# A hybrid decoder layer on one core: the GLA values' way into token rows, and two sets of loads

## The chip, the cores and the metric

The kernel runs on one core of one Trainium2 chip. The metric is the time of one launch on the device in microseconds (us); the median of the runs is compared. One execution was also recorded by the hardware profiler, and all times inside the kernel are from that one, counted from the start of its span. The engines are named as the profile names them: PE (TensorE's matmuls), PEld (its weight loads), DVE (VectorE), ACT (ScalarE), POOL (GpSimd) and SP (SyncE, which here only issues transfers).

## What is computed

One inference step of one layer of a hybrid decoder, for a prompt group (1 x 256 tokens) and a sample group (8 sequences x 4 tokens) that share all weights. The kernel keeps both groups side by side as T = 288 columns, so each weight is read once. Cut to what matters:

```python
p_mem_k, p_mem_v = _mem_kv(mem_prompt, norm_mem, w_ck, w_cv)     # 256 memory tokens, 4 heads x 512
xn = _rmsnorm(x, norm_mix)
z, xbc, dt_raw, q, k, v, r, g_lr, gate_a, gate_b = _split(xn @ w_in, IN_SIZES)
# branch a: causal conv and SSD scan of xbc (4 groups), gated by silu(z), normed, @ w_ssd_out
# branch b: GLA, 4 heads of 256 keys and 512 values, in chunks of tokens:
att = where(mask, einsum('bihk,bjhk->bhij', qe, ke), 0)
o = einsum('bhij,bjhv->bihv', att, v) + einsum('bihk,bhkv->bihv', qe, S)
S = exp(last) * S + einsum('bjhk,bjhv->bhkv', kd, v)
#           o normed, times silu(r), @ w_gla_out
merged = sigmoid(gate_a) * branch_a + sigmoid(gate_b) * branch_b
h = x + merged @ w_mix_out
h = h + cross_attend(rmsnorm(h), memory keys, memory values) @ w_co
h = h + (silu(gt) * a) @ w_down        # a, gt: causal conv of rmsnorm(h) @ w_up, 2 x 5632 channels
```

Outputs are y of both groups and the new states, memory keys and values among them.

## The kernel before

Everything is fp32. A projection (`proj_w`) streams its weights: SP loads 512 KB at a time into the tile `raw` (a ring of 3), ACT rounds it to `whi` (`wsplit`, L103), DVE takes the rest as `wlo` (L105; both rings hold WB = 5 tiles of two k-tiles each), and PE multiplies `whi` with the high and the low half of the activations and `wlo` with the high half (L147, L148, L151; 12 matmuls of 128x288 for a tile of weights and 256 output columns). Activations stand with channels on the partitions and tokens in the columns.

The kernel goes through these stages:

1. **Memory stage** (about the first 180 us). The memory's keys and values, one head of each at a time, by `mem_proj`: weights in `raw` as before, matmuls of 128x512 at L321, L322 and L325, 6 for a k-tile. The first of the eight projections also transposes the memory's rows. Over the next four (`w_cv` 0, `w_ck` 1, `w_cv` 1, `w_ck` 2, 64 k-tiles) `weave` runs a background, one of its steps for about each k-tile: `x_norm` (37 steps) and `x_prep`. `x_norm` loads the tokens x by `x_load(n)` (L387): n = 0 the sample group, 4 transfers of 64 KB; n = 1 to 4 each 64 tokens of the prompt, 4 transfers of 128 KB. They go through SP's queue, between the weights' loads. At step 12 and at every third step from 15 to 36 `square` reads one loaded piece on ACT and turns it on DVE (L396, L398).
2. **Eight units**: four SSD groups, then four GLA heads. The background of unit n is the scan of group or head n, and its main stream is the projections of unit n + 1 and the output projection of unit n - 1; the last unit's main stream is half of gate a. `weave` mixes them by step counts (`N_MAIN`, `N_BG`). `gla_proj` of head h makes `vT` (512 values x 288 tokens, four 128-row tiles, copied out of PSUM at L978) in the first 16 steps of the unit ahead. `gla_scan` needs the prompt's values with tokens on the partitions: per 128 tokens PE transposes four 128x128 blocks (L1068), ACT copies the PSUM tile twice (`vth`, `vt`) and DVE takes `vtl`. These feed the state update (L1132) and the output (L1140).
3. **Half gate**: gate b over all 16 tiles of channels. `gate_b(t)` combines gate, branch b (`mb`) and the merged half that lies in DRAM (`mar`, four tiles a load, a ring of 2; L1334 reads it). After every fourth tile it starts a load of keys for the cross-attention. The x that the next projection adds (`hx`, two tiles a load, a ring of 3) is loaded here too.
4. `w_mix_out`, cross-attention, `w_co`, and the ConvFFN, which fills the span from about 1590 us.

The transfers of stage 3, `vT`'s new ones and the states go through POOL's queue: POOL works through its instructions in order, and a transfer that waits for its buffer holds those behind it. So does SP. The order on each engine comes from a scheduler that works on the program as recorded; `keep_in_program_order` and the background's steps bind it.

The SSD scan already has what the change brings to GLA: `load_square` reads a state in pieces of 32 rows (four transfers of 64 KB, each in runs of 32 numbers) into `sqr`, and one DVE transpose (L881), which turns every 32x32 block by itself, finishes the turn.

Of the kernel before, what the change touches and what calls it, by code (L numbers as in the profile page):

```python
# [16 lines left out]
P = 128  # L17
D = 2048
KT = D // P
SEQ = 256  # L20
# [22 lines left out]
def hybrid_step(ctx: ExitStack, tc: tile.TileContext, I: dict, O: list):  # L43
# [22 lines left out]
    def mm_tile():  # L66
        return ps.tile([P, 512], F32, tag="mm", bufs=3, name="mm")
# [204 lines left out]
    with pool("p0") as p0:  # L272
# [118 lines left out]
        def x_norm():  # L391
            ss = p0.tile([P, 9], F32, name="ss")

            def square(b):
                junk = p0.tile([P, 512], F32, name="junk")
                tc.keep_in_program_order(S.activation(junk, xrow[:, b, :], ACT.Square, accum_out=ss[:, b:b + 1]))  # L396
                tc.keep_in_program_order(
                    V.transpose(xT[:, :, 32 * b:32 * b + 32], xrow[:, b, :].rearrange("p (x j) -> p j x", j=KT)))  # L398

            for step in range(37):  # L400
                if step == 3 or step % 6 == 0 and 6 <= step <= 24:
                    x_load(step // 6)
# [175 lines left out]

    def b2r(name):
        return pa.tile([P, 512], F32R, tag="b2", bufs=10, name=name)  # L580

    def r2(name):
        return pa.tile([P, 512], F32R, tag="r2", bufs=3, name=name)
# [390 lines left out]
    def gla_proj(h, out):  # L974
        vT, sr = a4("vT"), a4("sr")
        for j2 in range(2):
            def consv(j, a, j2=j2):
                S.copy(vT[:, 2 * j2 + j, :], a)  # L978
            yield from proj(I["w_in"], O_V + 512 * h + 256 * j2, 256, X, KT, consv)
        for j2 in range(2):  # L980
            def consr(j, a, j2=j2):
                silu2(a, sr[:, j2 * 2 + j, :])
# [57 lines left out]
        out.append((eb, qe, ke, kd, kde, vT, sr))  # L1040

    def gla_scan(h, eb, qe, ke, kd, kde, vT, sr):

        sq = pa.tile([P, T], F32, tag="sq", bufs=1, name="sqa")
        sins = []
# [15 lines left out]
        ksr = rep4(kd[:, :, SEQ:T], "ksr")  # L1061
        ker = rep4(ke[:, :, SEQ:T], "ker")

        vt = []
        for i in range(2):
            a = mm_tile()
            for t in range(4):
                TR(a[:, t * P:(t + 1) * P], vT[:, t, i * P:(i + 1) * P], ident)  # L1068
            vt.append((b2r("vth"), b2r("vtl"), b2("vt")))
            split(*vt[i][0:2], a)  # L1070
            S.copy(vt[i][2], a)
            yield

        a = mm_tile()
        for i, (t0, n) in enumerate(TOK):
            for k in range(2):
# [41 lines left out]
        kt = b2r("kth"), b2r("ktl")  # L1118
        split(*kt, a)
        yield  # L1120
        elp = pa.tile([P, 2], F32, tag="elp", bufs=1, name="elp")
        V.tensor_tensor(elp, eb[:, :, 191], eb[:, :, 255], ALU.mult)
        for k in range(2):
# [198 lines left out]
    pc_cm = pool("pc")  # L1322
    pc = pc_cm.__enter__()
    mas = []
    for q in range(4):
        m = pc.tile([P, 4, T], F32, tag="mar", bufs=2, name="mar")
        G.dma_start(out=m, in_=mg_d[:, 4 * q:4 * q + 4, :])
        mas.append(m)

    def gate_b(t, a):  # L1330
        th = pc.tile([P, T], F32, tag="th", bufs=3, name="th")
# [1 line left out]
        V.scalar_tensor_tensor(th, th, 1.0, mb[:, t, :], ALU.add, ALU.mult)  # L1333
        V.tensor_tensor(th, th, mas[t // 4][:, t % 4, :], ALU.add)  # L1334
        split_from(*mx(t), th, 0.5)
        if t % 4 == 3:
            key_load(0, t // 4, th[:, 0:1])

    hx = []

    def load_x(j2):
        m = pc.tile([P, 2, T], F32, tag="hx", bufs=3, name="hx")
        G.dma_start(out=m, in_=x_d[256 * j2:256 * j2 + 256].rearrange("(t p) n -> p t n", p=P))
        hx.append(m)

    for j2 in range(3):
        load_x(j2)
    run(gate(O_GB, gate_b))
    def sq_add(acc, ht, t):

# [512 lines left out]
```

## Time and profile before

| | |
|---|---|
| median of 3 runs | 2512.9 us (2511.34 to 2514.22) |
| the profiled execution's own time | 2508.11 us |
| its span, first to last instruction | 2506.4 us |
| mean granted TensorE clock | 0.999 |
| DVE, ACT, POOL busy | 71%, 54%, 16% |
| DMA | 524 MB, mean 209 GB/s |

The profile gives busy time by engine and by group of instructions (line, engine, operation, output<-input), what ended each engine's waits, and the chain of work that ended last, followed back from the end. Ends of matmuls are modelled, so PE counts as busy over the time in which results drain; the chain is the better measure of what a matmul costs, since its pieces follow each other without overlap. An engine's name with a q is its sequencer, which issues.

### The profile page before, as it was taken

To read this page: it belongs to the slowest core of one execution; us is meant where nothing else is said; L and a number is where in the kernel's file an instruction comes from. 1 tells how busy PE (TensorE), PEld (TensorE's weight loads), DVE (VectorE), ACT (ScalarE), POOL (GpSimd) and SP (SyncE) were. 2 spreads that over 40 slices of the span, in tenths; PEclk is the share of its full clock that TensorE was granted. 3 is DMA by queue.
4 is the path that set the end of the run, shared out by engine and by line. 5 is a ranking of instruction groups with operands and counts; after the bars stand their busy time and mean duration, and the time that the engine had idled before them with its cause. 6 is when DMAs were issued, how large, how long until landed. Compare 5 with 4: busy or idle time off the path is not lost.

```text
span 2506.4 us, 50377 instructions
## 1 busy us (share of the span) xinstructions
PE 2486.2 (99%) x18858; PEld 2400.7 (96%) x18858; DVE 1768.8 (71%) x3780; ACT 1341.4 (54%) x2725; POOL 407.7 (16%) x750
## 2 busy tenths in 40 slices
PE   9999999999999999999999999999999999999998
PEld 7889999999999999999999989999999999999998
DVE  6756777797877666776666577667777677675766
ACT  6655647656464656454555544555555455454545
POOL 3002133342300000010001122402111001020012
PEclk9999999999999999999999999999999999999999
DMA  8776587867858585767678598655555555555555
GB/s 249 242 221 196 172 250 207 234 192 236 233 187 286 182 254 175 249 218 262 200 227 272 191 321 323 205 162 178 170 171 170 170 169 171 169 172 170 170 173 170
DMA packets 443189, 524.31 MB, mean 209 GB/s; under 512 B 27404, under 2 KB 390764, under 8 KB 442912
## 3 DMA queue, kind: packets, MB, share of 16 engines
q1 hardware_dynamic: 408000, 422.34, 54.8%
q0 software_dynamic: 34912, 98.74, 12.3%
q8 instruction: 148, 2.42, 0.4%
q14 instruction: 97, 0.79, 0.1%
q10 hardware_dynamic: 32, 0.01, 0.0%
HBM read 474.31 MB, written 46.66 MB: 208 GB/s over the span
## 4 chain that ended last, share of the span: by engine, by line
PE 94%; DMA 2%; DVE 2%; issue 0%; ACT 0%; SPq 0%; POOL 0%; DVEq 0%; ACTq 0%
PE acc L148 28%; PE acc L147 27%; PE acc L151 27%; PE acc L321 2%; PE acc L322 2%; PE acc L325 2%; DMA raw<-in_w_cv_dram 1%; DVE wlo L105 1%; PE mm L1168 1%; PE la L1159 1%; PE la L1492 1%; DMA raw<-in_w_co_dram 0%; PE la L1550 0%; PE mm L1132 0%; PE la L867 0%
## 5 line engine op out<-in xcount | busy, mean ns | idle before, releaser
L103 ACT CAST whi<-raw 128x512 fp32r<-128x512 f32 x1464 | 896.3, 618 | 997.5 <-PE acc L148 762.2
L105 DVE TENSOR_TENSOR wlo<-raw,whi 128x512 fp32r<-128x512 f32 x1464 | 996.7, 687 | 579.6 <-ACT whi L103 565.9
L147 PE MATMUL acc<-xn,whi 128*128 128x288 f32 (+1 forms) x1936 | 544.5, 297 | 0.5 <-DVE sz L636 0.5
L148 PE MATMUL acc<-xn,whi 128*128 128x288 f32 (+1 forms) x1936 | 541.5, 295 | 0.0
L151 PE MATMUL acc<-xn,wlo 128*128 128x288 f32 (+1 forms) x1936 | 410.1, 293 | 0.0
L148 PE MATMUL acc<-hf,whi 128*128 128x288 f32 x1408 | 393.2, 296 | 0.0
L147 PE MATMUL acc<-hf,whi 128*128 128x288 f32 x1408 | 389.1, 292 | 0.0
L147 PEld LDWEIGHTS acc<-xn,whi 128*128 128x128 f32 (+1 forms) x1936 | 364.1, 188 | 8.0 <-issue 3.9
L148 PEld LDWEIGHTS acc<-xn,whi 128*128 128x128 f32 (+1 forms) x1936 | 364.2, 188 | 4.0 <-issue 1.7
L151 PEld LDWEIGHTS acc<-xn,wlo 128*128 128x128 f32 (+1 forms) x1936 | 310.4, 188 | 1.9 <-issue 0.8
L151 PE MATMUL acc<-hf,wlo 128*128 128x288 f32 x1408 | 294.8, 290 | 0.0
L148 PEld LDWEIGHTS acc<-hf,whi 128*128 128x128 f32 x1408 | 264.9, 188 | 0.1
L147 PEld LDWEIGHTS acc<-hf,whi 128*128 128x128 f32 x1408 | 264.2, 188 | 0.1
L151 PEld LDWEIGHTS acc<-hf,wlo 128*128 128x128 f32 x1408 | 226.3, 188 | 0.0
L148 PE MATMUL acc<-pr,whi 128*128 128x288 f32 x704 | 196.6, 296 | 0.0
L147 PE MATMUL acc<-pr,whi 128*128 128x288 f32 x704 | 194.8, 293 | 0.0
L151 PE MATMUL acc<-pr,wlo 128*128 128x288 f32 x704 | 147.4, 290 | 0.0
L147 PE MATMUL acc<-un,whi 128*128 128x288 f32 x512 | 143.7, 297 | 0.0
L148 PE MATMUL acc<-un,whi 128*128 128x288 f32 x512 | 143.2, 295 | 0.0
L1664 POOL COPY fsp<-fst 128x16 f32<-128x16 f32 x88 | 36.1, 413 | 657.1 <-DVE av L1676 433.5
L148 PEld LDWEIGHTS acc<-pr,whi 128*128 128x128 f32 x704 | 132.5, 188 | 0.0
L147 PEld LDWEIGHTS acc<-pr,whi 128*128 128x128 f32 x704 | 132.1, 188 | 0.0
(523 smaller groups left out, 4295.0 us busy)
## 6 DMA issues: line engine op xcount, KB each, us to landing
raw<-in_w_in_dram SPq DMA_DIRECT2D x240, 512.0 KB
raw<-in_w_up_dram SPq DMA_DIRECT2D x176, 512.0 KB
raw<-in_w_down_dram SPq DMA_DIRECT2D x88, 512.0 KB
raw<-in_w_cv_dram SPq DMA_DIRECT2D x32, 512.0 KB
raw<-in_w_ssd_out_dram SPq DMA_DIRECT2D x32, 512.0 KB
sin<-in_state_gla_dram POOLq DMA_DIRECT2D x32, 512.0 KB, 6.1
out_dram<-sin SPq DMA_DIRECT2D x32, 512.0 KB
raw<-in_w_gla_out_dram SPq DMA_DIRECT2D x32, 512.0 KB
```

The lines of the kernel that those rows point to most:

```text
L103: S.copy(hi, raw)
L105: V.tensor_tensor(lo, raw, hi, ALU.subtract)
L147: MM(a, hi[:, k, cs], xh, start=(k0 + s0 + k == 0), stop=False)
L148: MM(a, hi[:, k, cs], xl, start=False, stop=False)
L151: MM(a, lo[:, k, cs], xh, start=False, stop=(k0 + s0 + k == nk - 1))
L321: MM(accs[m], mn_hi[:, kk, ms_], hi[:, 0, :], start=(kk == 0), stop=False)
L322: MM(accs[m], mn_lo[:, kk, ms_], hi[:, 0, :], start=False, stop=False)
L325: MM(accs[m], mn_hi[:, kk, ms_], lo[:, 0, :], start=False, stop=(kk == KT - 1))
L1159: MM(osa[NS * j:NS * j + NS, :], qdm[:, k, b, :], sins[b][:, k, :], start=False, stop=(q == 1 and k == 0))
L1168: MM(a, kb[:, k * P:(k + 1) * P], vst, start=True, stop=True)
L1492: MM(ssc[NS * c:NS * c + NS, 0:P], xq[:, j, u, :], kt[:, j], start=(j == 0), stop=(j == 15))
L1664: G.tensor_copy(sp[:, :, 0:2], st.rearrange("p (b k) -> p b k", k=2))
```

## The change

Three edits. In the memory stage `x_load(0)` to `x_load(4)` stand at steps 5, 9, 15, 21 and 27 where they stood at 3, 6, 12, 18 and 24. In each GLA head, `vT`'s prompt half is written to DRAM (512 KB, one transfer) after its projection, read back as two tiles in eight transfers of 64 KB, each of 32 partitions with runs of 32 numbers, and turned on DVE in place; PE's transposes and ACT's plain copies go, and the split stands behind the key's instead of at the scan's start. In the half gate, `mar` 0 is loaded as before, `mar` 1 after gate tile 0, and 2 and 3 after tiles 3 and 7; `hx` 0 to 2 after tiles 5, 9 and 13. Each of these loads is tied by a POOL copy of one column of the gate tile into the buffer.

```diff
             for step in range(37):
-                if step == 3 or step % 6 == 0 and 6 <= step <= 24:
-                    x_load(step // 6)
+                if step in (5, 9, 15, 21, 27):
+                    x_load((step - 3) // 6)
...
+    def dumped(x, name):
+        d = dram.tile([4 * P, SEQ], F32, name=name)
+        G.dma_start(out=d.rearrange("(t p) n -> p t n", p=P), in_=x[:, :, 0:SEQ])
+        return d
+
+    def square_load(d, name):
+        got = []
+        for i in range(2):
+            t = b2(name)
+            rows = d.rearrange("(b p) (i q j) -> i q p b j", p=32, q=4, j=32)[i]
+            for q in range(4):
+                tc.keep_in_program_order(G.dma_start(
+                    out=t[32 * q:32 * q + 32].rearrange("p (b j) -> p b j", j=32), in_=rows[q]))
+            got.append(t)
+        return got
...
+        vd = dumped(vT, f"v_d{h}")
...
-        vt = []
-        for i in range(2):
-            a = mm_tile()
-            for t in range(4):
-                TR(a[:, t * P:(t + 1) * P], vT[:, t, i * P:(i + 1) * P], ident)
-            vt.append((b2r("vth"), b2r("vtl"), b2("vt")))
-            split(*vt[i][0:2], a)
-            S.copy(vt[i][2], a)
-            yield
-
+        vs = square_load(vd, "vt")
...
         split(*kt, a)
         yield
+        vt = []
+        for i in range(2):
+            V.transpose(vs[i], vs[i])
+            vt.append((b2r("vth"), b2r("vtl"), vs[i]))
+            split(*vt[i][0:2], vs[i])
+            yield
...
+    def load_mix(q, after=None):
         m = pc.tile([P, 4, T], F32, tag="mar", bufs=2, name="mar")
+        if after is not None:
+            G.tensor_copy(m[:, 0, 0:1], after)
         G.dma_start(out=m, in_=mg_d[:, 4 * q:4 * q + 4, :])
...
         split_from(*mx(t), th, 0.5)
+        if t == 0:
+            load_mix(1, th[:, 0:1])
         if t % 4 == 3:
+            if t < 11:
+                load_mix(t // 4 + 2, th[:, 0:1])
             key_load(0, t // 4, th[:, 0:1])
...
-    for j2 in range(3):
-        load_x(j2)
+        if t in (5, 9, 13):
+            load_x(t // 4 - 1, th[:, 0:1])
```

What becomes of the order, at three places. First SP's queue in the memory stage, from the first `w_cv` projection on; `raw` are weights, `xrow` the tokens. Before:

```order
L114 DMA raw<-in_w_cv_dram 128x2x512 x3
L387 DMA xrow<-in_x_sample_dram 32x512 x4
L114 DMA raw<-in_w_cv_dram 128x2x512
L387 DMA xrow<-in_x_prompt_dram 32x2x512 x4
L114 DMA raw<-in_w_cv_dram 128x2x512 x3
L387 DMA xrow<-in_x_prompt_dram 32x2x512 x4
L114 DMA raw<-in_w_cv_dram 128x2x512
L114 DMA raw<-in_w_ck_dram 128x2x512 x2
L387 DMA xrow<-in_x_prompt_dram 32x2x512 x4
L114 DMA raw<-in_w_ck_dram 128x2x512 x4
L387 DMA xrow<-in_x_prompt_dram 32x2x512 x4
```

And in the change:

```order
L114 DMA raw<-in_w_cv_dram 128x2x512 x4
L387 DMA xrow<-in_x_sample_dram 32x512 x4
L114 DMA raw<-in_w_cv_dram 128x2x512 x2
L387 DMA xrow<-in_x_prompt_dram 32x2x512 x4
L114 DMA raw<-in_w_cv_dram 128x2x512 x2
L114 DMA raw<-in_w_ck_dram 128x2x512
L387 DMA xrow<-in_x_prompt_dram 32x2x512 x4
L114 DMA raw<-in_w_ck_dram 128x2x512 x3
L387 DMA xrow<-in_x_prompt_dram 32x2x512 x4
L114 DMA raw<-in_w_ck_dram 128x2x512 x3
L387 DMA xrow<-in_x_prompt_dram 32x2x512 x4
```

Each x load went behind one to three more loads of weights: the sample group behind the fourth, the prompt's first behind the sixth where it stood behind the fourth, the last behind the fifteenth where it stood behind the fourteenth.

Second DVE at the start of the first GLA head's scan, where `vtl` is made. Before (`sz`, `un` are the end of the scan ahead, `qe` the head's query):

```order
L1028 SCALAR_TENSOR_TENSOR qe<-acc,eb 128x288
L191 SCALAR_TENSOR_TENSOR un<-sz,vcol,un 128x288
L105 TENSOR_TENSOR wlo<-raw,whi 128x512
L200 COPY qdm<-qe 128x8x4
L191 SCALAR_TENSOR_TENSOR un<-sz,vcol,un 128x288
L105 TENSOR_TENSOR wlo<-raw,whi 128x512
L200 COPY qdm<-qe 128x8x4
L105 TENSOR_TENSOR wlo<-raw,whi 128x512
L195 TENSOR_TENSOR vtl<-mm,vth 128x512
L105 TENSOR_TENSOR wlo<-raw,whi 128x512
L195 TENSOR_TENSOR vtl<-mm,vth 128x512
```

And in the change:

```order
L1131 STREAM_TRANSPOSE vt<-vt 128x512
L1045 SCALAR_TENSOR_TENSOR qe<-acc,eb 128x288
L191 SCALAR_TENSOR_TENSOR un<-sz,vcol,un 128x288
L105 TENSOR_TENSOR wlo<-raw,whi 128x512
L200 COPY qdm<-qe 128x8x4
L191 SCALAR_TENSOR_TENSOR un<-sz,vcol,un 128x288
L105 TENSOR_TENSOR wlo<-raw,whi 128x512
L200 COPY qdm<-qe 128x8x4
L105 TENSOR_TENSOR wlo<-raw,whi 128x512
L1131 STREAM_TRANSPOSE vt<-vt 128x512
L105 TENSOR_TENSOR wlo<-raw,whi 128x512
```

The two turns stand where the two `vtl` stood or a few instructions ahead; `vtl` itself went some 15 rows back, behind `ktl`. In the fourth head the first turn stands just ahead of the four `un` of the head before. On PE the eight groups of four transposes are gone, L1132's first products stand some 34 matmuls later in the first three heads, and the rest keeps its order.

Third POOL's queue at the fourth head's start, where `mq` (a part of gate a's half, four loads in all, each waiting for a buffer) stands. Before:

```order
L1049 DMA sin<-in_state_gla_dram 128x2x512 x3
L1227 DMA mq<-ma_d 128x576 x4
L1234 DMA mg_d<-mq 128x576
L1049 DMA sin<-in_state_gla_dram 128x2x512 x4
L1234 DMA mg_d<-mq 128x576
```

And in the change, where `v_d` is the head's copy of `vT` in DRAM:

```order
L1066 DMA sin<-in_state_gla_dram 128x2x512 x3
L1241 DMA mq<-ma_d 128x576 x3
L593 DMA vt<-v_d_12834 32x16x32 x8
L1241 DMA mq<-ma_d 128x576
L1248 DMA mg_d<-mq 128x576
L1066 DMA sin<-in_state_gla_dram 128x2x512 x4
```

The eight pieces stand between the third and the fourth load of `mq`. In the heads ahead they stand behind the last state load of the head before; in the first, behind the third of four loads of `gq`.

More of the change, by code (lines that the diff above doesn't have):

```diff
@@ L1039, in gla_proj, with gla_scan @@
         yield from proj(I["w_in"], O_Q + 256 * h, 256, X, KT, consq)
-        out.append((eb, qe, ke, kd, kde, vT, sr))
-    def gla_scan(h, eb, qe, ke, kd, kde, vT, sr):
+        out.append((eb, qe, ke, kd, kde, vT, sr, vd))
+    def gla_scan(h, eb, qe, ke, kd, kde, vT, sr, vd):
         sq = pa.tile([P, T], F32, tag="sq", bufs=1, name="sqa")
@@ L1324, in hybrid_step, with load_x @@
     mas = []
-    for q in range(4):
+    hx = []
+    def load_mix(q, after=None):
         m = pc.tile([P, 4, T], F32, tag="mar", bufs=2, name="mar")
+        if after is not None:
+            G.tensor_copy(m[:, 0, 0:1], after)
         G.dma_start(out=m, in_=mg_d[:, 4 * q:4 * q + 4, :])
         mas.append(m)
+    def load_x(j2, after=None):
+        m = pc.tile([P, 2, T], F32, tag="hx", bufs=3, name="hx")
+        if after is not None:
+            G.tensor_copy(m[:, 0, 0:1], after)
+        G.dma_start(out=m, in_=x_d[256 * j2:256 * j2 + 256].rearrange("(t p) n -> p t n", p=P))
+        hx.append(m)
+    load_mix(0)
     def gate_b(t, a):
@@ L1335, in gate_b @@
         split_from(*mx(t), th, 0.5)
+        if t == 0:
+            load_mix(1, th[:, 0:1])
         if t % 4 == 3:
+            if t < 11:
+                load_mix(t // 4 + 2, th[:, 0:1])
             key_load(0, t // 4, th[:, 0:1])
[L1339 to L1344, printed above, removed]
-    for j2 in range(3):
-        load_x(j2)
+        if t in (5, 9, 13):
+            load_x(t // 4 - 1, th[:, 0:1])
     run(gate(O_GB, gate_b))
```

## The prediction

> **What bounds the kernel now.** I read the page's first part and its chain first, then PE's own waits, then stretches around the three edits.
>
> ```profile
> PE 2486.2 (99%) x18858; PEld 2400.7 (96%) x18858; DVE 1768.8 (71%) x3780; ACT 1341.4 (54%) x2725; POOL 407.7 (16%) x750
> PE 94%; DMA 2%; DVE 2%; issue 0%; ACT 0%; SPq 0%; POOL 0%; DVEq 0%; ACTq 0%
> PE acc L321 <- ACT whi L103: 2.3, 3, 1.4
> L103 ACT CAST whi<-raw 128x512 fp32r<-128x512 f32 x1464 | 896.3, 618 | 997.5 <-PE acc L148 762.2
> ```
>
> PE is busy for 99% of the span and makes 94% of the chain; DMA makes only 2%. So an edit saves time only if it takes matmuls off PE or removes one of PE's few waits, and costs time only if it makes PE wait. Of those waits one row bears on the change: 2.3 us in three pieces at L321, the memory stage's matmuls, for rounded weights. The last row shows the cover elsewhere: ACT, which rounds the weights, sits idle 762.2 us because PE has not yet freed a buffer. ACT and DVE thus run ahead of PE by the ring of 5 tiles; a matmul of 288 columns costs 0.13 us (chain rows below), a tile takes 12 of them, 1.57 us, so four whole tiles are 6.3 us. A delay on DVE or ACT up to about that much is hidden, and beyond it is lost in full.
>
> **The GLA values, on PE.** These are the chain from 718.8 us (start, length), the group of all transposes, and the engines' busy time in two stretches of 20 us (after the length: PE, PEld, DVE, ACT, POOL; then granted clock, DMA share, GB/s).
>
> ```profile
> 718.77 0.26 PE acc L151 x2
> 719.04 0.44 PE mm L1068 x4
> 719.47 0.14 PE acc L147
> L1068 PE MATMUL mm<-ident,vT 128*128 128x128 f32 x32 | 4.8, 272 | 0.0
> 700.00:720.00 20.00, 20.00 (x157) 20.00 (x156) 17.59 (x45) 16.93 (x32) 0.00 (x0) 1.00 0.53 145
> 720.00:740.00 20.00, 20.00 (x157) 19.77 (x156) 14.02 (x32) 10.79 (x22) 3.43 (x5) 1.00 0.78 268
> ```
>
> Four transposes take 0.44 us of the chain, and the matmul behind them 0.14 instead of 0.13: 0.45 a group. 32 transposes are 8 groups: 8 x 0.45 = **-3.6 us**. The mean of 272 ns in the group's row includes the drain, which lies beside the next matmul, so I do not take 32 x 0.272 = 8.7 us; that stays as the far end. PE is busy for all of both stretches, so nothing waits for the transposes now: what they leave is filled by the next matmuls.
>
> The Trainium skill (TensorE: Matmul & The Clock Gate, section "Part 4: PE-mode transpose") gives about 275 ns for a 128x128 transpose in one kernel's context; the row's 272 agrees as a duration. As a price it would give 32 x 0.275 = 8.8 us instead of 3.6, but the chain has them start 0.11 apart.
>
> **The GLA values, beside PE.** DVE gains 8 turns; ACT loses 8 copies and POOL gets nine transfers a head. The nearest rows for a turn and for such transfers (busy, mean ns of an issue; KB each, us to landing), then the last state load of the first head and the second head's `vtl`:
>
> ```profile
> L881 DVE STREAM_TRANSPOSE st<-sqr 128x512 f32<-128x512 f32 x32 | 21.9, 697 | 0.0
> L730 POOL DMA_DIRECT2D sqr<-in_state_ssd_dram x128 | 82.8, 653 | 50.6 <-ACT ea L800 28.9 <-DVE st L881 10.9 <-DMA sin<-in_state_ssd_dram 6.8
> sqr<-in_state_ssd_dram POOLq DMA_DIRECT2D x128, 64.0 KB, 5.0
> vq<-in_cache_mem_v_dram POOLq DMA_DIRECT2D x16, 512.0 KB, 11.3
> h_d<-hx POOLq DMA_DIRECT2D x8, 288.0 KB, 5.0
> 778.31 0.72 POOL L1049 DMA_DIRECT2D sin<-in_state_gla_dram  x1 [3.16 <-DVE sin L1169]
> 841.34 0.68 DVE L195 TENSOR_TENSOR vtl<-mm,vth 128x512 fp32r<-128x512 f32 x1
> ```
>
> The turns are 8 x 0.697 = 5.6 us of DVE, 1.4 a head, beside PE and under the 6.3 us of cover: 0. The pieces have the form of `sqr`'s, and I price them so: 0.65 us to issue, 5.0 to land. Between that and 11.3, the slowest load on this queue, nothing changes so long as they are issued early. They are: the second head's stand behind the state load of 778.31, so they land by 779.0 + 8 x 0.65 + 5.0 = 789.2, and their turns stand where `vtl` ran at 841.3, 52 us later; the first and the third head's are placed alike. Uncovered, a late piece stalls DVE at its turn, behind which `wlo` is queued, and then PE. Neither end is below zero, since no wait of PE here is for what the loads replace. The write of `vT` has `h_d`'s row as nearest (5.0; 512 KB against 288), again far ahead of its reader. In the first GLA unit it stands on POOL ahead of the SSD states:
>
> ```profile
> 626.62 0.39 ACT L978 COPY vT<-acc 128x288 f32<-128x288 f32 x1
> 630.13 5.16 POOL L730 DMA_DIRECT2D sqr<-in_state_ssd_dram  x8 [28.95 <-ACT ea L800]
> ```
>
> The last copy of `vT` ends at 627.0; POOL has been waiting since before that for `ea` and issues at 630.1 anyhow. The write fits in: 0.
>
> The Trainium skill (DMA: Bandwidth & Descriptors, "Specifications") speaks against the pieces: below 512 bytes a transfer does a read-modify-write and misses line rate, and theirs are 128. `sqr`'s runs are 128 bytes too, and 64 KB of them take 5.0 us where a `sin` of 512 KB takes 6.1 (row below), so the price shows, though eight such loads overlap; by the rule the pieces move up towards the 11.3 end, which alters nothing before the fourth head.
>
> The fourth head is the tight one. POOL at its start, the DVE work before which the first turn now stands, and the state loads' landing:
>
> ```profile
> 1059.07 0.54 POOL L1227 DMA_DIRECT2D mq<-ma_d  x1 [36.83 <-DVE sin L1169]
> 1084.90 0.54 POOL L1227 DMA_DIRECT2D mq<-ma_d  x1 [25.30 <-DVE vtl L195]
> 1077.81 1.80 DVE L191 SCALAR_TENSOR_TENSOR un<-sr,rg,un 128x288 fp32r<-128x288 f32 x4
> sin<-in_state_gla_dram POOLq DMA_DIRECT2D x32, 512.0 KB, 6.1
> ```
>
> The pieces stand behind the third `mq` load. It waits 36.8 us for its buffer and goes at 1059.07, so they land by 1059.6 + 8 x 0.65 + 5.0 = 1069.8; the turn is due at 1077.8. 8 us to spare, or 2 by the 11.3 end: 0.
>
> **The memory stage.** PE at its two larger waits, then SP at the same places, which issues `raw` (weights) and `xrow` (tokens) in order:
>
> ```profile
> 44.33 0.61 PE L325 MATMUL acc<-wlo,mn_hi 128*128 128x512 f32 x2
> 46.32 0.51 PE L321 MATMUL acc<-whi,mn_hi 128*128 128x512 f32 x1 [1.38 <-ACT whi L103]
> ...
> 73.74 0.63 PE L325 MATMUL acc<-wlo,mn_hi 128*128 128x512 f32 x2
> 75.14 0.50 PE L321 MATMUL acc<-whi,mn_hi 128*128 128x512 f32 x1 [0.78 <-ACT whi L103]
> 33.54 1.80 SPq L387 DMA_DIRECT2D xrow<-in_x_sample_dram  x4
> 35.44 0.39 SPq L114 DMA_DIRECT2D raw<-in_w_cv_dram  x1
> 35.87 2.16 SPq L387 DMA_DIRECT2D xrow<-in_x_prompt_dram  x4
> 38.12 1.76 SPq L114 DMA_DIRECT2D raw<-in_w_cv_dram  x2
> 64.08 2.37 SPq L387 DMA_DIRECT2D xrow<-in_x_prompt_dram  x4
> 66.58 0.90 SPq L114 DMA_DIRECT2D raw<-in_w_ck_dram  x2
> 45.65 2.39 ACT L103 CAST whi<-raw 128x512 fp32r<-128x512 f32 x4 [3.46 <-DMA raw<-in_w_cv_dram]
> 35.00:57.00 22.00, 20.54 (x89) 16.32 (x88) 9.61 (x15) 9.71 (x19) 0.78 (x1) 1.00 1.03 289
> ```
>
> Matmuls of 512 columns start 0.23 apart (the pair at 44.33 is busy 0.61 with its drain), so PE was done at 44.8 and went on at 46.3: 1.5 us lost. At 73.74 likewise: done at 74.2, on at 75.1: 0.9 lost. At the first, ACT waits 3.46 us for `raw` issued from 38.12 on, behind two sets of x loads (1.80 and 2.16 us of issue). In the change the sample's set stands one `raw` later and the prompt's first two later. So the `raw` of 38.12 goes behind one set instead of two. By issue alone it gains the 2.16 of that set; I take 1.5, since its buffer may hold it a little. In bytes, 512 KB at the stretch's 289 GB/s are 1.8. Here it landed at 45.65 and PE went on 0.67 later; 1.5 earlier PE has it at 44.8, just when it needs it: **-1.5**. At the second place the prompt's third set (64.08) moves behind one more `raw`; one of the two loads that stood behind it (66.58) goes ahead, the other stays: I take half, **-0.4**. Bounds: 0, since x's bytes still have to come in, and the whole, 2.4.
>
> What comes late instead is x: two steps, about 2.7 us. `square` reads each piece nine steps after its issue, now seven by the step numbers, at 1.37 us a step (6 x 0.23): over 8 us, where a load of 512 KB lands in 6.1 (the `sin` row). Background work, behind no matmul that waits: 0.
>
> **The half gate.** Two stretches in columns as above, and POOL there:
>
> ```profile
> 1180.00:1200.00 20.00, 20.00 (x156) 20.00 (x155) 12.98 (x26) 7.77 (x13) 0.00 (x0) 1.00 0.89 289
> 1200.00:1220.00 20.00, 20.00 (x156) 20.00 (x156) 11.10 (x19) 9.52 (x17) 0.00 (x0) 1.00 0.60 168
> 1176.45 1.07 POOL L1327 DMA_DIRECT2D mar<-mg_d  x2
> mar<-mg_d POOLq DMA_DIRECT2D x4, 576.0 KB, 6.1
> L1334 DVE TENSOR_TENSOR th<-th,mar x16: 446/453/458, 1210.6 to 1299.7; 128x288 f32<-128x288 f32 x16
> ```
>
> The change takes one `mar` load (576 KB) and the three `hx` behind it out of the busy first stretch (289 GB/s), but PE has 156 matmuls in each stretch and no idle time: nothing to gain, 0. The loss: `mar` 1 now goes after gate tile 0, at about 1211, and lands by 1218; tile 4 asks at 1234 (16 tiles of L1334 between 1210.6 and 1299.7, 5.9 apart). `mar` 2 and 3 go after tiles 3 and 7 as their buffers demand. The third `hx` goes after tile 13, near 1288, lands by 1294 at `mar`'s 6.1, and is read only behind the whole gate: 0. If that cover were gone, a late `mar` would hold L1334 and the gate's tiles behind it, beyond the 6.3 us.
>
> **The sum**: -3.6 - 1.5 - 0.4 + 0 = -5.5. The profiled execution took 2508.11 (its span 2506.4 and 1.7 around it) and would take 2502.6; it lies 4.8 under the median, so the median goes from 2512.9 to **2507.4**. That is just over 0.2% (5.0 us), about what a measurement of this kernel can tell from no change; the limits are 2507.9 and 2517.9.
>
> **Rivals.**
> - *The memory waits only move.* For: DMA is at full share (1.03) from 35 to 57 us, where the waits stand, and the same bytes have to come. Against: the weights now go first in the queue. Then only the transposes: 2512.9 - 3.6 = 2509.3.
> - *Both memory waits go.* For: the third L321 wait is nearly nothing and later x loads leave gaps. -3.6 - 2.4 = -6.0, with a little from the third wait 2506.8.
> - *The pieces of the fourth head come late*, and it is slower. They are behind a load whose buffer decides. The third `mq` went at 1059.07, the fourth at 1084.90. If the change of buffers makes the third as late as the fourth, the pieces land at 1085.4 + 5.2 + 5.0 = 1095.7, 17.9 after the 1077.8 that is wanted; less the cover of 6.3, PE loses 11.6: 2507.4 + 11.6 = 2519.0. It begins to cost when that load goes after 1073.3, and ends slower than before from 1083.8 on. For: the ring of these buffers is shared with the split values. Against: its releaser, L1169, is the state update of the head before, which the change leaves in place.
> - *A transpose costs its whole duration*: -8.7 - 1.9 = -10.6, 2502.3. Against: the chain.
> - *The change does not do what it says on PE*: the 3.6 us that the transposes leave become waits for weights that come no earlier. For: DVE and ACT have 17.59 and 16.93 of 20 us busy from 700 on. Against: PE waits for neither there, and their load falls behind 720. Only -1.9: 2511.0.
>
> **How the numbers follow.** Forecast 0.45, of it 0.09 above 2507.9; waits only move 0.17; both go 0.13; fourth head late 0.10; full transposes 0.05; no gain on PE 0.10. Faster: 0.36 + 0.13 + 0.05 = 0.54; same: 0.09 + 0.17 + 0.10 = 0.36; slower: 0.10. The runs shown reach 1.6 below and 1.3 above their median. The range's top is the case without PE's gain and that scatter, 2511.0 + 1.3, rounded to 2512.5; its bottom takes in both waits gone and the scatter (2506.8 - 1.6 = 2505.2) and a fifth of the 5.1 open on the transposes: 2504.0. It leaves out the full transposes and the late head, 0.15, and tails of the rest.
>
> **What would show it.** L1068 gone from the chain, with PE still busy for all of 20 us in the stretches from 700 to 740. PE's row for L321 down from 2.3 us to about 0.4. No wait of DVE for `vt` by DMA; in the fourth head the pieces issued near 1060. From 1180 to 1220 still 156 matmuls in each 20 us. Wrong would be: L321 waits of the old size at other times, the pieces issued after 1073, or gate tiles waiting for `mar`.

## The result and the profile after

The changed kernel took 2506.89 us (median of 11 runs, 2503.55 to 2510.27) against 2512.9 of the kernel before (2507.63 to 2516.66): ratio 0.9978, 95% interval 0.9968 to 0.9987. (The ratios are estimated from the runs of both kernels and are not quite the quotients of the two medians.) The forecast was 2507.4. The sum came out; its terms did not all, and one of them was wrong in kind, as the experiments below show.

The page's first part of the changed kernel, its chain, and PE's waits (total, times, longest):

```profile
span 2501.7 us, 50398 instructions
PE 2482.8 (99%) x18826; PEld 2397.9 (96%) x18826; DVE 1770.3 (71%) x3788; ACT 1333.0 (53%) x2717; POOL 439.4 (18%) x792
PE 95%; DMA 2%; DVE 1%; issue 1%; POOL 0%; ACT 0%; SPq 0%; DVEq 0%; ACTq 0%; POOLq 0%
PE mm L909 <- ACT cst L618: 3.0, 1, 3.0
PE mm L1810 <- DVE h L1776: 1.2, 1, 1.2
PE mm L358 <- DVE epsc L78: 1.1, 1, 1.1
```

PE lost 32 matmuls and 3.4 us of busy time, the span 4.7. The L321 row is gone from the waits altogether, where 0.4 us had been forecast. The longest wait now is one of 3.0 us at L909, in an SSD group, which the change does not touch; it was 1.7 before.

The stretches of the prediction once more, in the changed kernel (length; busy time and instructions of PE, PEld, DVE, ACT, POOL; clock, DMA share, GB/s):

```profile
35.00:57.00 22.00, 22.00 (x99) 18.11 (x98) 11.20 (x17) 10.41 (x21) 0.78 (x1) 1.00 0.97 286
57.00:69.00 12.00, 12.00 (x55) 9.94 (x54) 8.17 (x12) 8.33 (x18) 0.73 (x1) 1.00 0.93 295
69.00:76.00 7.00, 7.00 (x33) 5.79 (x32) 5.74 (x9) 4.68 (x11) 0.00 (x0) 1.00 0.90 257
700.00:720.00 20.00, 20.00 (x159) 20.00 (x157) 17.59 (x48) 15.97 (x30) 0.00 (x0) 1.00 0.57 160
720.00:740.00 20.00, 20.00 (x153) 19.74 (x153) 14.14 (x31) 9.86 (x20) 3.40 (x5) 1.00 0.82 278
1180.00:1200.00 20.00, 20.00 (x157) 20.00 (x156) 11.78 (x22) 8.06 (x13) 0.00 (x0) 1.00 0.62 176
1200.00:1220.00 20.00, 20.00 (x156) 20.00 (x155) 13.23 (x25) 11.14 (x21) 2.17 (x5) 1.00 0.68 195
```

From 35 to 57 us PE ran 99 matmuls where it ran 89, without idle time, at nearly the same GB/s. From 1180 to 1200 the DMA share fell from 0.89 to 0.62 with PE as busy as ever; that looked like the nothing that was forecast. SP's queue in the memory stage, and POOL's at the fourth head with the turns' group and the pieces' landing:

```profile
32.90 1.57 SPq L114 DMA_DIRECT2D raw<-in_w_cv_dram  x2
34.58 1.79 SPq L387 DMA_DIRECT2D xrow<-in_x_sample_dram  x4
36.47 2.57 SPq L114 DMA_DIRECT2D raw<-in_w_cv_dram  x2
39.09 2.26 SPq L387 DMA_DIRECT2D xrow<-in_x_prompt_dram  x4
```

```profile
1053.77 0.54 POOL L1241 DMA_DIRECT2D mq<-ma_d  x1 [38.79 <-DVE sin L1183]
1054.30 0.68 POOL L593 DMA_DIRECT2D vt<-v_d  x1
1055.81 4.51 POOL L593 DMA_DIRECT2D vt<-v_d  x7 [0.83 <-issue]
1072.51 0.71 DVE L1131 STREAM_TRANSPOSE vt<-vt 128x512 f32<-128x512 f32 x1
L1131 DVE STREAM_TRANSPOSE vt<-vt x8: 705/708/718, 716.7 to 1077.4; 128x512 f32<-128x512 f32 x8
vt<-v_d POOLq DMA_DIRECT2D x32, 64.0 KB, 5.2
```

The second pair of weights now goes at 36.47, right behind one set of x. The fourth head's pieces were issued by 1060.3; with the median landing time of 5.2 us they were there at 1065.5, 7 us before their turn at 1072.5 (the longest landing time of any piece, 8.2 us, would leave 4). A turn takes 0.71 us against the 0.697 taken from `sqr`'s row, and no wait of DVE stands before one of the eight.

### Where the time went, stage by stage

PE runs its projection matmuls in the same order in every kernel here but for a few exchanged neighbours (24 of some 16,750 in e7_hold, 53 in the three kernels with a copy moved to DVE), so the n-th of them can be compared: its start in a trace less its start in the trace of before. The table has how much that difference grows from one place to the next (times of the kernel before; minus is time gained). Between the listed places the differences stay constant to 0.1 us or so: time is won and lost at a few spots only. The runs are told below, e7_hold by itself.

| trace | memory, 40 to 500 | SSD's end, 545 to 690 | GLA, 690 to 1130 | half gate and mix, 1170 to 1420 | 1420 to 2440 |
|---|---|---|---|---|---|
| changed kernel | -3.71 | +1.77 | -4.24 | +1.30 | +0.25 |
| e9_after, the same again | -2.52 | +2.27 | -4.23 | +2.76 | +0.17 |
| e1_gla | -0.19 | +1.51 | -4.23 | +8.26 | +0.86 |
| e2_mem | -1.81 | +3.18 | 0.00 | 0.00 | +0.34 |
| e3_half | -1.60 | +3.97 | 0.00 | +2.09 | +0.16 |
| e4_no_tr | +0.30 | -0.04 | -3.65 | +0.25 | +0.60 |
| e5_x_pool | +0.54 | +3.46 | 0.00 | 0.00 | +1.59 |
| e6_x_later | -1.08 | +0.23 | -4.24 | +0.95 | -1.01 |
| e8_cst | -1.32 | +0.63 | -4.23 | +0.63 | +1.17 |
| e10_cst | +0.49 | -0.68 | -4.23 | +2.43 | +0.80 |
| e11_no_x | -3.74 | -0.12 | -4.24 | +1.78 | -0.75 |
| e12_two | -1.42 | +1.72 | -4.23 | +8.67 | +0.20 |

The GLA column does not scatter at all; every other column does, by up to 2 us between two executions of one kernel, and "SSD's end" by up to 4 between kernels that are alike there. One trace's total therefore proves little; a column's values over several traces prove more.

The scatter in "SSD's end" comes mostly from a single place. PE waits there for one small copy on ACT (L893 in the kernel before, L909 in the changed one): 1.6 to 4.5 us in the traces where the copy is on ACT. In e9_after, e2_mem, e3_half and e5_x_pool the granted clock right behind that wait is 0.50 for 3.4 us; the wait of 3.0 us in the changed kernel's first trace is followed by no such stretch. In e9_after:

```profile
567.00:569.00 2.00, 2.00 (x10) 2.00 (x9) 0.59 (x1) 0.62 (x1) 0.99 (x2) 0.50 1.26 321
```

### The profile page after: what moved, and what is told of

Read it like the earlier page. It is cut to its first block, busy times and chain, and to the rows that moved or that the text cites. A ratio compares the mean times of both kernels' runs of the same rounds, so it can differ in the third digit from the quotient of the medians.

```text
span 2501.7 us, 50398 instructions
## 1 busy us (share of the span) xinstructions
PE 2482.8 (99%) x18826; PEld 2397.9 (96%) x18826; DVE 1770.3 (71%) x3788; ACT 1333.0 (53%) x2717; POOL 439.4 (18%) x792
## 4 chain that ended last, share of the span: by engine, by line
PE 95%; DMA 2%; DVE 1%; issue 1%; POOL 0%; ACT 0%; SPq 0%; DVEq 0%; ACTq 0%; POOLq 0%
PE acc L148 27%; PE acc L147 27%; PE acc L151 27%; PE acc L321 2%; PE acc L325 2%; PE acc L322 2%; PE mm L1182 1%; PE la L1173 1%; PE la L1516 1%; PE la L1574 0%; PE mm L1146 0%; DMA sqr<-in_state_ssd_dram 0%; DMA raw<-in_w_in_dram 0%; DMA kc<-in_cache_mem_k_dram 0%; DVE wlo L105 0%
```

## The experiments

**The three edits apart.** `e1_gla` is the kernel before with the GLA edit alone, `e2_mem` with this alone:

```diff
-                if step == 3 or step % 6 == 0 and 6 <= step <= 24:
-                    x_load(step // 6)
+                if step in (5, 9, 15, 21, 27):
+                    x_load((step - 3) // 6)
```

and `e3_half` with the half gate's loads tied to gate tiles alone, as in the change:

```diff
+        if t == 0:
+            load_mix(1, th[:, 0:1])
         if t % 4 == 3:
+            if t < 11:
+                load_mix(t // 4 + 2, th[:, 0:1])
             key_load(0, t // 4, th[:, 0:1])
...
-    for j2 in range(3):
-        load_x(j2)
+        if t in (5, 9, 13):
+            load_x(t // 4 - 1, th[:, 0:1])
```

> Only the GLA values' edit, the rest as before. Forecast theory: PE loses eight groups of 0.45 us and nothing else moves, -3.6 us of 2512.9 (ratio 0.9986), and PE's drift against the kernel before grows from 0 to about -3.6 between 720 and 1095 us. Rival, a transpose costs its whole 272 ns: -8.7 (0.9965). Rival, the freed time turns into waits for weights: 0 (1.000).

> Only the later loads of x. Forecast: first wait of PE at L321 gone, second halved, -1.9 us (ratio 0.9992). Rival, both waits go: -2.4 (0.9990). Rival, read off the changed kernel's trace, where PE is 3.7 us ahead by 140 us: -3.7 (0.9985). Rival, the waits only move: 0 (1.000), with waits of together 2.3 us at L321 at other times.

> Only the half gate's loads tied to gate tiles. Forecast: 0 (ratio 1.000), PE idle nowhere from 1176 to 1400 us. Rival, read off the changed kernel's trace, where PE loses about 1.1 us between 1360 and 1380 us, while the loads of x for the next projection are added: +1.1 (1.0004), with that loss at the same matmuls here.

Measured: e1_gla 2510.42 us, ratio 0.9994 (0.9982 to 1.0006); e2_mem 2509.48, 0.9987 (0.9975 to 0.9999); e3_half 2511.75, 0.9991 (0.9981 to 1.0001), against 2512.6 of before on the same chip. None is decided by its time. By the table, the GLA edit gives 4.23 us between 690 and 1130, more than forecast and half of the 8.7 of the full-duration rival. But e1_gla then loses 8.26, at a place that the edit does not touch. These are ACT, which rounds weights, and PE in e1_gla:

```profile
1186.49 1.14 ACT L103 CAST whi<-raw 128x512 fp32r<-128x512 f32 x2 [5.54 <-DMA raw<-in_w_gla_out_dram]
1188.95 0.37 PE L147 MATMUL acc<-un,whi 128*128 128x288 f32 x1 [0.60 <-ACT whi L103]
```

and two stretches of e1_gla, then the first of them in the changed kernel:

```profile
1175.00:1185.00 10.00, 10.00 (x79) 10.00 (x78) 5.59 (x11) 2.38 (x4) 1.65 (x3) 1.00 1.03 375
1200.00:1220.00 20.00, 20.00 (x151) 20.00 (x150) 10.52 (x18) 9.42 (x17) 0.00 (x0) 1.00 0.61 166
```

```profile
1175.00:1185.00 10.00, 10.00 (x79) 10.00 (x78) 7.09 (x14) 3.72 (x6) 0.00 (x0) 1.00 0.75 233
```

In e1_gla the loads of `mar` and `hx`, which stand at about 1173 to 1177 as they did before, fill DMA (share 1.03, 375 GB/s). ACT waits 5.5 us for the weights behind them (3.7 in the kernel before), and PE waits 0.6 us. After that wait PE runs 151 matmuls in 20 us instead of 156, at a granted clock of 1.00 and with no idle time, from 1189 to 1414. The starts of successive projection matmuls are 134.4 ns apart there and 130.0 in the kernel before. 4.4 ns over some 1700 matmuls are 7.5 us, which with the 0.8 us that PE's starts lose at the wait itself make the 8.3. In the changed kernel the same stretch has a DMA share of 0.75, and no wait.

The row puts PE's wait down to ACT, whose cast happens to end at the same moment. But the tile of weights that PE takes next had been rounded at 1187.11, and its `wlo` was done at 1187.83, both before PE wanted it at 1188.2. What was missing is the accumulator: two pairs of `acc` buffers are used in turn, and the pair whose turn it is comes free when DVE has added it to `mb`. DVE takes its work in order and had stood at `wlo` for 4.5 us, because the weights were late. DVE in e1_gla, then at the same place in the kernel before:

```profile
1187.14 1.29 DVE L105 TENSOR_TENSOR wlo<-raw,whi 128x512 fp32r<-128x512 f32 x2 [4.53 <-ACT whi L103]
1188.35 0.81 DVE L984 TENSOR_TENSOR mb<-acc,mb 128x288 f32<-128x288 f32 x2
```

```profile
1189.33 1.29 DVE L105 TENSOR_TENSOR wlo<-raw,whi 128x512 fp32r<-128x512 f32 x2 [2.81 <-ACT whi L103]
1190.54 0.82 DVE L968 TENSOR_TENSOR mb<-acc,mb 128x288 f32<-128x288 f32 x2
```

In e1_gla the first of the two `mb` ends at 1188.80 and PE goes on at 1188.95, 0.15 us later. In the kernel before PE's first matmul in the freed buffer starts 0.49 us after that `mb`: it was 0.34 us short of the same wait.

**The transposes without what replaces them.** `e4_no_tr` leaves the transposes out and puts nothing in their place, so its GLA values are wrong:

```diff
-            a = mm_tile()
-            for t in range(4):
-                TR(a[:, t * P:(t + 1) * P], vT[:, t, i * P:(i + 1) * P], ident)
+            a = vT[:, :, i * P:(i + 1) * P]
```

> The kernel before with the 32 transposes left out and nothing in their place: the split and the copy read the untransposed values, so the GLA heads compute with wrong values; no write to DRAM, no pieces, no turns. Forecast: the same -3.6 us as the GLA edit alone (ratio 0.9986), since the edit's traffic and turns were priced at 0. Rival, traffic and turns cost something: this one is faster than the GLA edit alone by that much, and its PE drift from 720 to 1095 us the larger.

Measured: 2508.68, 0.9983 (0.9970 to 0.9997). Its GLA column is -3.65: the 8 x 0.45 = 3.6 of the prediction, shown by itself. The edit gains 0.58 more than that, so its traffic and turns cost nothing that shows, and the moved order gives something besides. Summing PE's starts over this stretch by kind, a projection matmul is followed by a group of the scan 128 times in the kernel before, 120 times in e4_no_tr and 119 times in e1_gla: one group more has joined a neighbour (0.23 us), and the q-k products take 0.24 less. The rest of the 0.58 is spread thinly.

**x's place in the queue, or its bytes.** `e5_x_pool` is the kernel before with x's loads on POOL's queue, `e6_x_later` the changed kernel with them later still, and `e11_no_x` the changed kernel with a constant written to `xrow` instead, so that it computes from wrong tokens:

```diff
-                tc.keep_in_program_order(nc.sync.dma_start(
+                tc.keep_in_program_order(nc.gpsimd.dma_start(
```

```diff
-                if step in (5, 9, 15, 21, 27):
-                    x_load((step - 3) // 6)
+                if step in (8, 12, 18, 24, 30):
+                    x_load((step - 6) // 6)
```

```diff
-                tc.keep_in_program_order(nc.sync.dma_start(
-                    out=xrow[32 * i:32 * i + 32, b:b + m, :],
-                    in_=src[:, 512 * i:512 * i + 512].rearrange("(b t) d -> t b d", t=32)))
+                tc.keep_in_program_order(G.memset(xrow[32 * i:32 * i + 32, b:b + m, :], 1.0))
```

> The kernel before, with the loads of x at their old steps but issued by POOL instead of SP, so the same bytes come at about the same time and only stand in no weights' way in the queue. Forecast theory, the place in SP's queue makes the waits at L321: they go, and PE is some 2.4 us ahead of the kernel before at 140 us (2510.5, ratio 0.9990). Rival, DMA's full share makes them: waits of about 2.3 us stay at L321, 2512.9 (1.000).

> The changed kernel with the loads of x three more steps later (steps 8, 12, 18, 24, 30), so that each is read 3 steps, some 4.1 us, after its issue instead of 6, some 8.2. Forecast theory, x is behind no wait of PE because it lands in time: now it lands late, the squares wait on ACT and hold the weights' rounding behind them, and PE loses up to 2 us a set once the tiles ahead are used up: waits of 1 to 6 us at L321 (2508 to 2513). Rival, the loads' landing has more room than that: as the changed kernel, 2506.9 (0.9978).

> The changed kernel with the tokens' loads left out (a constant is written in their place, so everything behind is computed from wrong tokens): no x transfers at all in the memory stage. If x's bytes make what is left of the waits there, PE is idle for less than 0.2 us from 20 to 145 us, some 0.8 to 1.5 less than the changed kernel's traces on average. If the weights' own transfers make it, L321 still waits for 0.5 to 1.5 us.

Measured: e5_x_pool 2516.67, 1.0023 (1.0011 to 1.0035); e6_x_later 2505.86, 0.9975 (0.9965 to 0.9986); e11_no_x 2503.04, 0.9971 (0.9958 to 0.9985). Two stretches of the kernel before, then of e11_no_x:

```profile
20.00:60.00 40.00, 38.54 (x175) 31.03 (x174) 23.75 (x47) 24.79 (x54) 4.18 (x12) 1.00 0.86 248
60.00:100.00 40.00, 39.22 (x172) 31.87 (x171) 25.45 (x37) 22.84 (x47) 1.45 (x2) 1.00 0.83 254
```

```profile
20.00:60.00 40.00, 40.00 (x185) 32.88 (x184) 25.74 (x48) 26.50 (x58) 8.61 (x16) 1.00 0.68 221
60.00:100.00 40.00, 40.00 (x178) 33.08 (x177) 27.99 (x44) 25.39 (x51) 11.74 (x13) 1.00 0.82 266
```

PE's idle time is the length less its busy time: 1.46 and 0.78 before, nothing without x. The same for the other traces, with 100 to 140 us added to the second stretch:

| x's loads | PE idle 20 to 60 | PE idle 60 to 140 |
|---|---|---|
| old steps (before, e1, e3, e4) | 1.46, 1.35, 1.61, 2.11 | 0.94, 0.90, 0, 0.93 |
| new steps (changed, e2, e7, e8, e9, e10) | 0, 0.39, 0, 0.23, 0.76, 1.09 | 0, 0.60, 0.78, 1.36, 0, 1.39 |
| old steps, POOL's queue (e5) | 1.62 | 1.16 |
| three steps later still (e6) | 0 | 1.47 |
| none (e11) | 0 | 0 |

The first wait shrinks from a mean of 1.63 to 0.41: -1.2. The second stretch has a mean of 0.69 either way: nothing gained. Busy time includes the drain of the last matmul before a wait, so idle time counts a wait short; by PE's starts the same traces give -1.5 for the first stretch and nothing (+0.15) for the second. With x's loads on POOL the weights stand behind no x in SP's queue, and 1.62 us of waits stay, in three pieces. So x's bytes delay the weights from another queue too; a place ahead of them in SP's queue isn't needed for that. Whether the place adds something isn't shown, since POOL issued the first three sets between 31.8 and 40.3, and SP the same three between 33.5 and 45.3. e5_x_pool is also slower than the kernel before, by some 4.7 us, which neither of its forecasts has. In its trace the memory stage has 0.5 of that; the rest stands in "SSD's end" and behind 1420, places that scatter in every kernel, and why it is slower isn't shown. e6_x_later shows that the squares have more room than its forecast gave them: three steps are enough, and ACT nowhere waits for x.

**How long DVE may be held.** `e7_hold` is the changed kernel with one long instruction behind the first turn of heads 1 to 3:

```diff
             V.transpose(vs[i], vs[i])
+            if i == 0 and h:
+                held = pa.tile([P, 24], F32, tag="held", bufs=1, name="held")
+                tc.keep_in_program_order(V.tensor_reduce(
+                    held[:, 0:8 * h], vs[i].unsqueeze(1).to_broadcast([P, 8 * h, 512]), AX.X, ALU.add))
```

> The changed kernel with one long DVE instruction more in the second, third and fourth GLA head, three instructions behind the first turn: a reduction over 8, 16 and 24 times 512 numbers, some 4.3, 8.5 and 12.8 us at the turn's pace; its result is not used. Forecast theory, DVE can be held for 6.3 us there and PE loses what goes beyond: 0, 2.2 and 6.5 us, together 8.7 (ratio of the before 1.0013). Rival, PE waits there for DVE work other than the weights' rest too: nearly the whole hold is lost, together some 20 to 25 us (1.006). Rival, DVE runs further ahead than the four tiles: together under 4 (0.9994).

Measured: 2526.77, 1.0060 (1.0044 to 1.0076). The holds, PE's waits for `wlo` in all, the one after the longest hold, and a stretch behind the shortest:

```profile
L1134 DVE TENSOR_REDUCE held<-vt x3: 4404/8670/12941, 838.5 to 1091.4; 128x8 f32<-128x4096 f32 x1, 128x16 f32<-128x8192 f32 x1, 128x24 f32<-128x12288 f32 x1
PE acc L151 <- DVE wlo L105: 17.8, 4, 9.9
1105.00 1.33 PE L151 MATMUL acc<-xn,wlo 128*128 128x288 f32 x4 [9.86 <-DVE wlo L105]
845.00:851.00 6.00, 6.00 (x30) 6.00 (x29) 5.88 (x18) 1.14 (x2) 0.00 (x0) 0.50 0.86 253
```

Against the changed kernel, PE lost 6.9 us over the head with the hold of 4.4, 8.7 over that with 8.7, and 11.6 over that with 12.9: 27.1 together, where 8.7 was expected. The theory of a cover of 6.3 us fell. The trace of the kernel before shows why: between the end of a tile's `wlo` and PE's first matmul with it lie at least 2.56, 3.25, 3.25 and 3.77 us in the four heads (2.56, 3.45, 3.44 and 3.45 in the changed kernel), not 6.3. The time is that of the rival by which nearly the whole hold is lost (1.006), but not for its reason: in these heads all waits but one of 0.5 us are for `wlo`. The waits in the rows come to some 18 us. Most of the rest is the clock: after each of the three waits the granted clock is 0.50 instead of 1.00, and PE works at half pace, its matmuls of 288 columns 0.24 us apart instead of 0.13, for 6.8, 5.7 and 2.8 us. Half of that, an estimate of 7.6 us, makes 25 to 26 of the 27.1; the last 1 to 2 us are not accounted for. So a hold of 4.4 us cost 6.9: 2.2 of waiting for `wlo`, some 3.4 of half pace behind it, and smaller things.

**The changed kernel again, and the wait at L909.** `e9_after` is the changed kernel unaltered. `e8_cst` and `e10_cst` are the same kernel twice, the changed one with this in `conv_cache`:

```diff
-        S.copy(st[0:108], a[0:108, 0:P])
+        V.tensor_copy(st[0:108], a[0:108, 0:P])
```

> The changed kernel with the copy that ends PE's longest wait in its trace (3.0 us at L909 for a 108x128 copy on ACT that stands behind two casts, which wait for weights) put on DVE. Theory, the copy's place on ACT costs the wait: it shrinks by 1 to 2 us (2505.5). Rival, the weights are late there anyway and PE waits as long at the next projection's matmul: 2506.9. The memory stage and the GLA heads are the changed kernel's, so PE's gain there, 3.7 and 4.2 us in its first trace, is taken once more: forecast of the prediction 1.9 and 3.6.

> The changed kernel unaltered, beside the next two on one chip. If its gain is -1.5 in the memory stage's first wait and -4.2 in the GLA heads, as the traces so far have it, and the rest scatters: ratio 0.9977, PE idle from 20 to 60 us under 0.4, and a drift of -4.2 between 690 and 1130 us. If the first result was a lucky draw: 0.9985 or above.

> The changed kernel with the 108x128 copy on DVE once more, beside the changed kernel itself. If the copy's place on ACT cost a wait of 1.5 to 4.5 us at L909, this one is 1.5 to 3 us faster than the changed kernel; if the wait only moves to the next one, which its first trace suggests (2.1 us for sz at the next projection), the same within 1 us.

Measured: e8_cst 2503.64, 0.9969 (0.9958 to 0.9979); e9_after 2507.59, 0.9990 (0.9977 to 1.0004); e10_cst 2503.99, 0.9969 (0.9956 to 0.9982). The last two ran on one chip, where the kernel before took 2509.62. The repetition's interval holds the first result and also no change; its stage columns are the first trace's, memory -2.52 for -3.71. The copy on DVE is the fastest version that does all of the work, some 3.5 us under the changed kernel: on the one chip 12 runs of each have medians 3.6 apart. The wait moves rather than goes, as this row of e10_cst has it:

```profile
PE acc L147 <- DVE sz L652: 2.1, 1, 2.1
```

so the column "SSD's end" is only some 1 us better (+0.63, -0.68 and, below, +1.72, against a mean of 1.5 with the copy on ACT). In e8_cst the clock is at 0.50 for 3.4 us behind the moved wait, and in e10_cst it is not: around that wait the two lose 2.93 and 1.53 us. What makes up the other 2 us of the lead isn't shown.

**Without the half gate's edit.** `e12_two` is e8_cst with the loads of `mar` and `hx` put back to where they stood before:

```diff
-    load_mix(0)
+    for q in range(4):
+        load_mix(q)
...
-        if t in (5, 9, 13):
-            load_x(t // 4 - 1, th[:, 0:1])
+    for j2 in range(3):
+        load_x(j2)
```

> The changed kernel with the half gate's loads put back as they were before, and with the 108x128 copy on DVE. Theory, the half gate's edit costs 0.6 to 2.8 us, because its loads meet the keys' and the weights come late at single tiles between 1250 and 1400 us (all eight traces that have the edit lose that much there, four of the five without it under 0.3): here PE's drift from 1170 to 1420 us is within 0.3 of nothing, and the time is 1 to 2 us under that of the changed kernel with the copy on DVE (2503.6 and 2504.0 of before's 2511.9 and 2509.6, ratio 0.9969): 0.9963. Rival, the loss there comes by chance whatever the edit, as in the one trace of 8.3 us without it: drift 0.6 or more here too, 0.9969.

Measured: 2507.65, 0.9985 (0.9974 to 0.9996), beside 2511.94 of before: some 4 us slower than e8_cst and e10_cst, not 1 to 2 faster. The theory fell. Its rival had a loss of 0.6 or more in this stretch right, but not the time; the loss is 8.67, e1_gla's 8.3 us over again:

```profile
1175.00:1185.00 10.00, 10.00 (x79) 10.00 (x78) 4.38 (x9) 2.15 (x4) 0.45 (x1) 1.00 1.02 361
1188.14 0.37 PE L147 MATMUL acc<-un,whi 128*128 128x288 f32 x1 [1.01 <-ACT whi L103]
1200.00:1220.00 20.00, 20.00 (x151) 20.00 (x150) 11.08 (x19) 9.23 (x18) 0.00 (x0) 1.00 0.59 168
```

The same full DMA, a wait at the same tile (1.01 us), and again 134.4 ns a matmul until 1413. PE again goes on 0.15 us after the `mb` that frees its accumulator. That time, from the `mb` to PE's first matmul in the freed buffer, is at its least 0.15 us in e1_gla, e12_two and e4_no_tr, 0.29, 0.30 and 0.49 in e5_x_pool, e2_mem and the kernel before, and over 2.1 in all eight traces with the new half gate. So all six traces with the old half gate wait there or are within 0.4 us of it, with the GLA edit or without. In e4_no_tr, which has no GLA edit, PE's starts slip at two such places, by 0.25 us together. What only the two traces with the GLA edit have is the slower beat behind the wait. That it never follows without the edit isn't shown: e4_no_tr's 12 runs lie as far apart (2502.04 to 2516.30) as e1_gla's (2506.55 to 2517.20).

The new half gate has a smaller price of its own: all eight traces with it, e7_hold among them (+0.60), lose 0.6 to 2.8 us between 1250 and 1400. In e9_after this is the place:

```profile
1261.00 0.53 PE L151 MATMUL acc<-xn,wlo 128*128 128x288 f32 x2 [0.66 <-DVE wlo L105]
1280.00:1300.00 20.00, 20.00 (x154) 20.00 (x153) 15.93 (x30) 10.44 (x21) 4.52 (x4) 1.00 0.66 208
```

A wait of 0.66 us, and after it 154 matmuls in 20 us (131.7 ns each) until 1407. `mar`, `hx` and the keys now come one behind the other from 1205 to 1295, and single tiles of weights arrive late.

## Why the prediction was right, and which of its steps were not

- *The sum.* -5.5 was forecast. By the columns: GLA -4.2, the memory stage's first wait -1.2 to -1.5, the second 0; the half gate between its own price of 0.6 to 2.8 and the 8 that it spares where the burst strikes. The measured 6.0 is not these terms added up exactly, since SSD's end and the memory stage scatter by some 2 us from one execution to the next. That it came within 0.5 us of the forecast is luck: the repetition gave 2.0 and an interval that holds no change.
- *GLA values on PE, -3.6.* Right, and shown alone at -3.65 by e4_no_tr. The transposes cost their starts, 0.11 us each, and not their 272 ns. By the figure of about 275 ns of the Trainium skill (TensorE: Matmul & The Clock Gate, "Part 4: PE-mode transpose") as a price, 8.8 us, e4_no_tr would have gained more than twice what it did. The edit's -4.23 has 0.58 more from groups that joined.
- *GLA beside PE, 0.* Right in its result. The reason given, 6.3 us of cover, was wrong: the least slack is 2.6 to 3.8, and e7_hold, held for 26.0 us in all, lost 27.1. A turn of 0.71 us is well inside the least slack, and the split that went back makes room; that this is why the turns cost nothing is argued, not shown by a run of its own.
- *The fourth head.* Right: pieces at 1054.3 to 1060.3, there 7 us ahead by the median landing time.
- *The memory stage, -1.5 and -0.4.* The first wait is right in size: -1.2 by idle time, -1.5 by PE's starts, which is how it was forecast. The second term failed: taking half of the wait at 75.1 us took it for a fixed place, and it is one that comes in some executions and not in others, 0.69 us on average with the old steps and the new. The reason, x's place ahead of the weights in SP's queue, isn't borne out: on POOL's queue x's bytes make waits as large. The set issued at 64.08 is the prompt's fourth, not its third, which alters no term. The squares' lead was put at seven steps; for the prompt's sets it is six, and three are enough.
- *The half gate, 0.* This step failed. "PE has 156 matmuls in each stretch and no idle time: nothing to gain" reads the trace of a kernel in which the burst just did not delay PE: the accumulator came free 0.34 us before PE would have waited for it. In e1_gla, e12_two and e4_no_tr the same burst held PE up, and in the two of them with the GLA edit 225 us of slower matmuls follow. Between e12_two and e8_cst or e10_cst, which differ in this edit alone, the ratios differ by 0.0016, 4.0 us, though their intervals just overlap and e12_two ran on another chip. Why the slower beat follows the wait with the GLA edit and not in e4_no_tr isn't shown.

## What to carry to other kernels

Where an engine is busy without a gap, look at the slack that its suppliers have there before pricing a burst at nothing: a stretch that shows no wait may be 0.3 us short of one. Count everything that the engine needs, not its inputs alone: here late weights held up DVE, and PE then lacked a free accumulator while its weights were ready. A cover is to be measured as the least time between a product's end and its first use over the stretch, not as the size of the ring, and a wait can cost more than its length, since PE may be slower behind it. And a wait seen once in a stage where DMA is full is a draw, not a term: what a move of loads gains there takes several traces to size.

## What the runs showed of the hardware

Behind a wait PE can be slower in two ways, and neither follows every wait.

*The granted clock.* In e7_hold it falls to 0.50 after waits of 2.2 to 9.9 us, and the matmuls then start 0.24 us apart instead of 0.13. In e9_after, e2_mem, e3_half and e5_x_pool (waits of 2.5 to 4.5 us) and in e8_cst and e12_two (2.1) it is 0.50 for 3.4 us, in the changed kernel (3.0) and e10_cst (2.1) not at all. What decides it isn't shown.

*A slower beat at full clock.* After a wait of 1.0 us or less (in e3_half one that shows only as 0.13 us more between two starts) PE can go on at a slower beat for as long as it has no further gap. The projections' matmuls (128x288) then start 131.7 or 134.4 ns apart on average instead of 130.0, with the granted clock at 1.00 and no idle time shown; it ends at the next group of other matmuls (1407 to 1414 here). Seen from 1189 in e1_gla and 1188 in e12_two (134.4), from 1268 in e3_half and 1260 in e9_after (131.7), and in shorter pieces elsewhere. It cost some 7 us in e1_gla and e12_two and under 2 in the other two. Why the beat locks in at these values isn't shown.
